# A planner's counts for transfers, instruction fetches and waiting margins are replaced in a hybrid attention layer on one core

## The chip, the cores and the metric

The kernel runs on one core of a Trainium2 chip. The metric is the device time of one execution in microseconds, taken as the median of several runs. The core has a matrix engine (PE in the profile, with PEld for the loading of its stationary operand), a vector engine (DVE), a scalar engine (ACT), a general engine (POOL) and a queue engine (SP) that issues the transfers. Each engine works through its own list of instructions in the order in which the program lists them; between engines they wait on semaphores.

## The reference, cut to what matters

The input x has 512 tokens of 1024 channels. One RMS norm and one wide projection feed two attention mixers and their gates; both mixers are projected, merged with sigmoid gates and projected once more.

```python
h = rms_norm(x, norm_w[l])
proj = h @ w_in[l]
(q_a, k_a, v_a, z_a, q_b, kc, vc, ksl, vsl, kwn, vwn, gate_b, z_b, gate_m) = jnp.split(proj, ...)
o_a = moba_mixer(rms_norm(heads(q_a), ...), rms_norm(heads(k_a), ...), heads(v_a), bias_a)
k_cmp = rms_norm(compress(heads(kc), cmp_pos_k[l], cmp_w1_k[l], cmp_w2_k[l]), k_norm_cmp[l])
v_cmp = compress(heads(vc), cmp_pos_v[l], cmp_w1_v[l], cmp_w2_v[l])
o_b = nsa_mixer(rms_norm(heads(q_b), ...), k_cmp, v_cmp, ksl, vsl, kwn, vwn, gate_b, bias_b)
y_a = o_a * jax.nn.silu(z_a)
y_b = o_b * jax.nn.silu(z_b)
merged = sigmoid(g_m[..., :1024]) * (y_a @ w_branch_a[l]) + sigmoid(g_m[..., 1024:]) * (y_b @ w_branch_b[l])
x = x + merged @ w_out[l]
```

Mixer A (MoBA) has 8 heads of 64 channels; with 512 tokens its two key blocks are both always taken, so that it is causal attention with a bias that depends on the distance. Mixer B (NSA) has 8 heads in 2 groups with three branches: attention to 31 compressed key blocks (`compress` is a two-layer network with 2048 inputs and 256 hidden units), to selected blocks and to a sliding window; here, too, all eight blocks are always selected and the window covers the whole sequence. The three are summed with sigmoid gates.

## The kernel before, in words

**Arithmetic.** Each float32 operand of a large product is split into a high and a low part. A product is three matmul passes: high by high, low by high, high by low. A weight tile of 128x512 comes by a transfer from SP (`dma`, L238) into a raw buffer `wr` (`NRAW` = 6 of them), ACT casts it to the high part `wh` (L402), and DVE subtracts to get the low part `wl` (L412). This is `Stream.split`; the chain of the two steps is listed from the moment at which the planner expects the raw tile to have landed. A second stream of the same class, `W1`, brings the 16 tiles of the compression network (`vh`, `vl`) through two raw buffers.

**Stages.** The projection is worked in pieces: token-major ones with psum tiles `pgt` and channel-major ones with `pgc`, all through `mm3` (matmul at L437). Then come the branch products (`pbr`) and the output products (`po`), through `mm3` as well.

**Attention.** There are 24 units (a pair of heads of one mixer or branch), each with 4 score blocks of up to 512 columns. A score block is two fp16 matmuls into one of two psum buffers `sps` (L1092, L1094). DVE adds the bias and accumulates the maximum (L1114, a custom instruction and a read of the accumulator into `sst`), ACT takes the exponential and the sum (L1125, L1127), DVE takes the reciprocal (L1128), ACT and DVE scale and split into fp16 parts (L1132, L1136), SP sends them through a transposing transfer (`dma_transpose`, L245) into `dst`, and PE multiplies with the values into `O` (24 matmuls, L1168; two more at L1304 add the compressed branch).

**Compressed branch.** The compressed keys and values are gathered from `pgc` (`X`, L912), split into `xs` (L724, L725), and multiplied with the W1 tiles into `hps` (L940). ACT copies the sum to `hs` (L947), PE transposes it into `pu` (L952), and after the second layer the compressed scores `scp` (L1252) follow, with their own softmax `sc` on DVE and ACT (L1257 to L1278, a maximum in `cm` at L1268) and a transpose `pct` (L1291). This happens twice for scores, once for each group of heads.

**The planner.** The order of the instructions on every engine is not written by hand. While the program is built, Python code emulates a clock `now[0]` and times at which each resource is free: `free["A"]`, `free["D"]`, `free["P"]` for the three elementwise engines, `free["S"]` for SP, `free["Q"]` for the transfer engines. Each piece of elementwise work is a `Chain` in a heap, listed when its emulated time comes. PE work comes from ten generators (`Run`): `A` for the score blocks, `O_` and `Y` for the value products and the sides before the output, `F` for the large products, `C` for the compressed branch, `B`, `V`, `Z`, `X`, `U` for preparation. A generator yields either a cost in emulated ns or a readiness; a run may go ahead when its readiness plus its margin (`MARGIN`, or `LATE_A`, `LATE_V`, `LATE_S`, `LATE_C`, `LATE_O`) has passed in the emulated clock, and when none may, the one that has been ready longest goes. Among those eligible, the least served by its share goes. Nothing of this exists on the chip: the chip sees lists of instructions and the semaphores between them. If a wait is real that the planner took to be over, PE stands still, and all that is listed behind stands with it.

The costs that the planner uses for transfers are in `dma` (L236 to L241) and `dma_transpose` (L243 to L247). The matmuls are issued at L437 (`mm3`), L699, L940, L952, L1092, L1094, L1168, L1252, L1304 and a few others, and the planner knows nothing of the fetching of instructions.

Of the kernel before, what the change touches and what calls it, by code (L numbers as in the profile page):

```python
# [108 lines left out]
def hybrid_kernel(ctx: ExitStack, tc: tile.TileContext, x, x0, xT, wtok, wchan, gains, w1,  # L109
# [126 lines left out]
    def dma(dst, src, n, t=None):  # L236

        nc.sync.dma_start(out=dst, in_=src)  # L238
        t = issue(now[0] if t is None else t, 420)
        free["Q"] = max(free["Q"], t + 1000) + max(450, n * P / 360)  # L240
        return free["Q"] + 1700  # L241

    def dma_transpose(dst, src, blocks):  # L243

        nc.sync.dma_start_transpose(out=dst, in_=src)  # L245
        free["Q"] = max(free["Q"], issue(now[0], 1230) + 1500) + blocks * 170
        return free["Q"] + 500  # L247
# [88 lines left out]
    class Stream:  # L336
# [48 lines left out]
        def split(w, upto):  # L385
            for i in range(w.next, min(upto, len(w.tiles))):
                w.next = i + 1
                if isinstance(w.tiles[i], Sum):
                    if i not in w.chain:
                        w.split_sum(i)  # L390
                    continue
                while i not in w.raw:
# [4 lines left out]
                w.out[i] = hi, lo
                c = w.chain[i] = Chain(max(now[0], t))

                def f(e, hi=hi, raw=raw):  # L400
                    if e is nc.scalar:
                        e.copy(hi, raw)  # L402
# [9 lines left out]
                c.do(either(n), lambda e, hi=hi, lo=lo, raw=raw: e.tensor_sub(lo, raw, hi.bitcast(F32))).mark((w, 1, i))  # L412
                c.call(w.load)
# [12 lines left out]
    def mm3(dst, sts, mvs, rows=1, start=True, stop=True, more=False, passes=((0, 0), (1, 0), (0, 1))):  # L426
# [3 lines left out]
        for k in range(0, n, rows):  # L430
# [4 lines left out]
            for a, b in passes:  # L435
                for i in ks:
                    nc.tensor.matmul(dst, sts[i][a], mvs[i][b], start=(start and i == a == b == 0),  # L437
                                     stop=(stop and i == n - 1 and (a, b) == passes[-1]), skip_group_check=more)
# [111 lines left out]
    def x_rms():  # L550
# [5 lines left out]
        for t in range(NT):  # L556
            nc.tensor.matmul(ps[:, t:t + 1], sq_sum[:, t * P:(t + 1) * P], ones, start=True, stop=True)
# [25 lines left out]
    def x_rows():  # L583
# [4 lines left out]
        for i in range(2):  # L588
            nc.tensor.matmul(ps, onesr, dg[i], start=(i == 0), stop=(i == 1))
# [24 lines left out]
    def v_scale(name, tag):  # L614
# [7 lines left out]
        nc.tensor.matmul(ps[:, :1], onesr.bitcast(F32), z[:, KT:KT + 1], start=True, stop=True)  # L622
# [194 lines left out]
    def proj_norm(name, first=False, tags="gggg"):  # L817
        two = []

        def emit(t, ps):  # L820
# [7 lines left out]
            if name == "kb":  # L828
                e_ = sp.tile([P, 24], F32, name=nm("ge"), tag="ge", bufs=3)
# [38 lines left out]
    def bias_rows():  # L868
# [5 lines left out]
        nc.tensor.matmul(ps, *oh, start=True, stop=True)  # L874
# [55 lines left out]
    def compress_h(kv):  # L930
# [4 lines left out]
        for q in range(8):  # L935
            ws = W1.take(1, 256)
            for z in range(2):
                yield ws[0][2].ready
                for i in range(2):
                    nc.tensor.matmul(hps[:, :256], st[2 * q + i], ws[i][z], start=(q == i == z == 0),  # L940
# [10 lines left out]
        for a in range(2):  # L951
            nc.tensor.matmul(ub[:, a * 64:(a + 1) * 64], hs[:, a * P:(a + 1) * P], ii, start=True, stop=True)  # L952
# [51 lines left out]
    def compress_v2(G):  # L1004
        yield room("t")
        ps = psum("t", "pv2")
        for g in range(2):
            for a in range(2):
                nc.tensor.matmul(ps[:, g * 64:(g + 1) * 64], G[:, 2 * a + g].rearrange("p r c -> p (r c)"),
# [31 lines left out]
    class Unit:  # L1041
# [36 lines left out]
        def qk(u, b):  # L1078
# [11 lines left out]
            for x in range(2):  # L1090
                if two:
                    nc.tensor.matmul(sps[:, :n].rearrange("p (h n) -> p h n", h=2), qs, k4[:, x, :, 0], start=not x, stop=bool(x))  # L1092
                else:
                    nc.tensor.matmul(sps[:, :n].rearrange("p (t n) -> p t n", n=P), qs, k4[:, x, j, :b + 1], start=not x, stop=bool(x))  # L1094
# [46 lines left out]
    class Pair:  # L1141
# [15 lines left out]
        def pv(p):  # L1157
# [5 lines left out]
            for kb in (0, 3, 2, 1):  # L1163
                n = S - kb * P
                for vi, pi in ((0, 0), (1, 0), (0, 1)):
                    for r, u in enumerate(p.us):
                        out = o[DH * r:DH * r + DH, S - n:].rearrange("p (b q) -> p b q", q=P)
                        nc.tensor.matmul(out, v[r][kb][:, vi * DH:(vi + 1) * DH], u.moving(kb, pi),  # L1168
# [65 lines left out]
    def nsa_units(g):  # L1234
# [8 lines left out]
        def pre1():  # L1243
# [3 lines left out]
            for i in range(4):  # L1247
# [3 lines left out]
                for b in range(NT):  # L1251
                    nc.tensor.matmul(sps[:, b * DH:(b + 1) * DH], q[:, b * S:b * S + P], kcs[:, g],  # L1252
# [45 lines left out]
        for j in range(2):  # L1298
            def before(o, j=j):
# [3 lines left out]
                for z in range(2):  # L1303
                    nc.tensor.matmul(o, vz[g][:, z].rearrange("p i d -> p (i d)"), ch, start=False, stop=bool(z))  # L1304
# [443 lines left out]
```

## Time and profile before

| | us |
|---|---|
| median of 3 runs | 421.62 |
| the 3 runs | 420.22, 421.62, 422.57 |
| profiled execution | 422.54 |
| its span (first to last instruction) | 420.5 |

| engine | busy us | share of the span |
|---|---|---|
| PE | 411.8 | 98% |
| PEld | 322.0 | 77% |
| DVE | 356.3 | 85% |
| ACT | 297.9 | 71% |
| POOL | 35.1 | 8% |

The engines' busy times overlap, so they do not add up to the span. Matmuls run in a pipeline and their ends are modelled; a short wait between two of them can vanish from the busy time of PE, so the idle times put down to PE and PEld in front of an instruction are read beside the busy share. The granted clock of PE was full in all 40 slices. The 16 transfer engines were busy for 70.5% of the span with the kernel's own transfers.

### The profile page before, as it was taken

The numbers are of one execution on the slowest core, as the hardware profiler recorded it, in microseconds if no ns is written. First come the engines' busy times: TensorE is split into PE (matmuls) and PEld (weight loads), VectorE is DVE, ScalarE is ACT, GpSimd is POOL, SyncE is SP. The second block draws the span as 40 slices with busy tenths as digits, with TensorE's granted clock in tenths as the row PEclk, the third lists the DMA queues.
The fourth block names the chain that finished last, engine by engine and source line by source line (L and its number), as shares of the span: only waits on it lengthen the run. The fifth ranks groups of instructions, "written<-read, shape, count | busy, mean of one in ns | idle before, by whom it ended". The sixth has DMA issues, their size and how long they took to land.

```text
span 420.5 us, 7307 instructions
## 1 busy us (share of the span) xinstructions
PE 411.8 (98%) x2235; PEld 322.0 (77%) x2235; DVE 356.3 (85%) x933; ACT 297.9 (71%) x793; POOL 35.1 (8%) x37
## 2 busy tenths in 40 slices
PE   9999998999998999999999999999999999999996
PEld 7877875778976677897766777666777888888885
DVE  5967969999899987778999997899956967698993
ACT  7996748997797988727988897898943433445620
POOL 0015100123210033200000000000000000000000
PEclk9999999999999999999999999999999999999999
DMA  8951785688969988750878778889799597251232
GB/s 278 311 190 49 129 271 140 137 183 214 264 201 232 195 163 194 218 153 12 147 168 196 150 161 200 167 195 160 145 162 348 175 374 278 79 180 44 56 143 100
DMA packets 116693, 75.30 MB, mean 179 GB/s; under 512 B 89072, under 2 KB 92016, under 8 KB 116656
## 3 DMA queue, kind: packets, MB, share of 16 engines
q1 hardware_dynamic: 116656, 74.86, 70.5%
q8 instruction: 17, 0.28, 0.3%
q14 instruction: 20, 0.16, 0.1%
HBM read 51.11 MB, written 2.75 MB: 128 GB/s over the span
## 4 chain that ended last, share of the span: by engine, by line
PE 54%; DVE 23%; DMA 9%; ACT 5%; issue 5%; SPq 1%; POOL 1%; DVEq 0%; ACTq 0%; POOLq 0%
PE pgc L437 21%; PE pbr L437 9%; PE po L437 9%; PE pgt L437 8%; DMA wr<-in_wtok 5%; DVE sb L1114 4%; DVE wl L412 4%; DVE sb L1136 4%; DMA wr<-in_w 3%; PE O L1168 3%; PE sps L1094 3%; ACT wh L402 2%; DVE vl L412 1%; SPq L238 1%; DMA T<-rtab 1%
## 5 line engine op out<-in xcount | busy, mean ns | idle before, releaser
L437 PE MATMUL pgc<-hh,wh 128*128 128x512 f32 x208 | 87.1, 419 | 0.0
L412 DVE TENSOR_TENSOR wl<-wr,wh 128x512 fp32r<-128x512 f32 (+1 forms) x112 | 73.1, 669 | 11.8 <-ACT wh L402 11.6
L437 PE MATMUL pgc<-hh,wl 128*128 128x512 f32 x208 | 81.5, 392 | 0.0
L437 PE MATMUL pgc<-hl,wh 128*128 128x512 f32 x208 | 81.2, 390 | 0.0
L402 ACT CAST wh<-wr 128x512 fp32r<-128x512 f32 (+1 forms) x111 | 64.0, 599 | 11.2 <-DMA wr<-in_wtok 5.6
L1125 ACT ACTIVATE sb<-sb,sst 128x256 f32<-128x256 f32 (+3 forms) x96 | 53.2, 554 | 10.5 <-DVE sst L1114 10.2
L437 PE MATMUL pgt<-wh,hh 128*128 128x512 f32 (+2 forms) x160 | 58.3, 364 | 0.1
L437 PE MATMUL pgt<-wl,hh 128*128 128x512 f32 (+2 forms) x160 | 56.1, 351 | 0.5 <-DVE wl L412 0.4
L437 PE MATMUL pgt<-wh,hl 128*128 128x512 f32 (+2 forms) x160 | 55.8, 349 | 0.0
L1136 DVE SCALAR_TENSOR_TENSOR sb<-sb,sst 128x256 f16<-128x256 f32 (+3 forms) x96 | 51.1, 542 | 4.2 <-ACT sb L1132 3.9
L1114 DVE CUSTOM_DVE_ANT_0 sb<-sps,T,gst 128x512 f32<-128x512 f32 (+3 forms) x96 | 51.2, 541 | 3.5 <-PE sps L1094 1.6
L1132 ACT ACTIVATE sb<-sb,sst 128x256 f16<-128x256 f32 (+3 forms) x96 | 51.4, 552 | 4.0 <-DVE sst L1128 3.7
L437 PEld LDWEIGHTS pgc<-hh,wh 128*128 128x128 f32 x208 | 39.1, 188 | 8.6 <-issue 0.3
L437 PEld LDWEIGHTS pgc<-hh,wl 128*128 128x128 f32 x208 | 39.0, 188 | 8.6
L437 PEld LDWEIGHTS pgc<-hl,wh 128*128 128x128 f32 x208 | 39.2, 189 | 6.5
L1094 PE MATMUL sps<-qkt,qkt 128*128 128x512 f16 (+3 forms) x176 | 38.2, 310 | 1.6 <-DVE sst L1114 1.4
L489 POOL TENSOR_TENSOR nr<-nss,mhalf 128x8 f32<-128x8 f32 (+1 forms) x16 | 29.0, 1819 | 109.4 <-DVE nss L488 47.9
L437 PEld LDWEIGHTS pgt<-wl,hh 128*128 128x128 f32 x160 | 30.1, 188 | 5.5 <-DVE wl L412 1.6
L437 PEld LDWEIGHTS pgt<-wh,hh 128*128 128x128 f32 x160 | 30.2, 189 | 4.3 <-DVE X L912 0.4
L437 PEld LDWEIGHTS pgt<-wh,hl 128*128 128x128 f32 x160 | 30.2, 189 | 3.4
L1094 PEld LDWEIGHTS <-qkt 128*128 128x128 f16 x176 | 11.5, 98 | 21.4 <-issue 18.5
L437 PE MATMUL pbr<-yh,wh 128*128 128x512 f32 x64 | 26.4, 413 | 0.0
(229 smaller groups left out, 746.3 us busy)
## 6 DMA issues: line engine op xcount, KB each, us to landing
wr<-in_wchan SPq DMA_DIRECT2D x52, 256.0 KB, 3.8
wr<-in_wtok SPq DMA_DIRECT2D x36, 256.0 KB, 4.0
wq<-in_wout SPq DMA_DIRECT2D x36, 256.0 KB, 3.1
T<-rtab SPq DMA_DIRECT2D x16, 256.0 KB, 4.0
wr<-in_w SPq DMA_DIRECT2D x16, 256.0 KB, 3.7
wr<-in_wbr SPq DMA_DIRECT2D x16, 256.0 KB, 3.1
xr<-in_x SPq DMA_DIRECT2D x8, 256.0 KB, 5.3
x<-in_xT SPq DMA_DIRECT2D x7, 256.0 KB, 5.8
```

Of the source, the lines that this page charges most:

```text
L238: nc.sync.dma_start(out=dst, in_=src)
L402: e.copy(hi, raw)
L412: c.do(either(n), lambda e, hi=hi, lo=lo, raw=raw: e.tensor_sub(lo, raw, hi.bitcast(F32))).mark((w, 1, i))
L437: nc.tensor.matmul(dst, sts[i][a], mvs[i][b], start=(start and i == a == b == 0), stop=(stop and i == n - 1 and (a, b) == passes[-1]), ski ...
L489: c.do({"p": 700 + 150 * w}, lambda e: e.tensor_tensor(v(dst), v(ss), mhalf[:parts, :w], op=ALU.pow))
L1094: nc.tensor.matmul(sps[:, :n].rearrange("p (t n) -> p t n", n=P), qs, k4[:, x, j, :b + 1], start=not x, stop=bool(x))
L1114: e.tensor_tensor_reduce(z["sb"], sps[:, :L], T[:, S - L:], scale=nrunscale, scalar=3e38, op0=ALU.add, op1=ALU.min, accum_out=st[:, 0, b:b ...
L1125: c.do({"A": 279 + 0.834 * L}, lambda e: e.activation(z["sb"], z["sb"], AF.Exp, bias=st[:, 0, b:b + 1], scale=-1.0, accum_out=st[:, 1, b:b ...
L1132: e.activation(z["pp"][:, :L], z["sb"], AF.Copy, scale=s_)
L1136: c.do({"d": 59 + cd(L)}, lambda e: e.scalar_tensor_tensor(z["pp"][:, L:], z["sb"], s_, z["pp"][:, :L], op0=ALU.mult, op1=ALU.subtract))
L1168: nc.tensor.matmul(out, v[r][kb][:, vi * DH:(vi + 1) * DH], u.moving(kb, pi), start=p.first and kb == vi == pi == 0, stop=p.last and kb == ...
```

## The change

The change alters numbers of the planner, one helper around the matmul, and the shape and count of one small tile. No instruction is added or removed: each engine issues as many of each kind as before, in another order. All matmuls go through the new helper `mm`, so that they share one line (L261), and lines behind it move down by 17 (L412 becomes L429, L1114 becomes L1131, L1136 becomes L1153, L912 becomes L929).

```diff
-MARGIN = 300
-LATE_A = 1000
+MARGIN = 450
+LATE_A = 750
 LATE_V = 2000
 LATE_S = 1000
-LATE_C = 300
+LATE_C = 1000
 LATE_O = 1000
-LATE_Y = 1000
+LATE_Y = 2000
...
+SQ_L = 560
+SQ_T = 1330
+DQ_L = 1540
+DE_L = 800
+DQ_T = 1370
+DE_T = 1200
+FETCH = 1200
+LAND = 500
+LAND1 = 1500
...
     def dma(dst, src, n, t=None):
 
         nc.sync.dma_start(out=dst, in_=src)
-        t = issue(now[0] if t is None else t, 420)
-        free["Q"] = max(free["Q"], t + 1000) + max(450, n * P / 360)
-        return free["Q"] + 1700
+        t = issue(now[0] if t is None else t, SQ_L)
+        free["Q"] = max(free["Q"], t + DQ_L) + max(300, n * P / 314)
+        return free["Q"] + DE_L
 
     def dma_transpose(dst, src, blocks):
 
         nc.sync.dma_start_transpose(out=dst, in_=src)
-        free["Q"] = max(free["Q"], issue(now[0], 1230) + 1500) + blocks * 170
-        return free["Q"] + 500
+        free["Q"] = max(free["Q"], issue(now[0], SQ_T) + DQ_T) + blocks * 145
+        return free["Q"] + DE_T
+
+    fetched = [0]
+
+    def mm(*a, **k):
+        nc.tensor.matmul(*a, **k)
+        fetched[0] += 2
+        if (fetched[0] + 90) % 256 < 2:
+            free["Q"] = max(free["Q"], now[0]) + FETCH
...
-                c = w.chain[i] = Chain(max(now[0], t))
+                c = w.chain[i] = Chain(max(now[0], t + (LAND1 if w is W1 else LAND)))
...
-                    nc.tensor.matmul(dst, sts[i][a], mvs[i][b], start=(start and i == a == b == 0),
+                    mm(dst, sts[i][a], mvs[i][b], start=(start and i == a == b == 0),
...
-                e_ = sp.tile([P, 24], F32, name=nm("ge"), tag="ge", bufs=3)
+                e_ = sp.tile([P, 34], F32, name=nm("ge"), tag="ge", bufs=4)[:, :24]
```

The replacement of `nc.tensor.matmul` by `mm` stands at all the other matmuls, too. In words: SP's time for one issue is counted as 560 instead of 420 ns (1330 instead of 1230 for a transposing one); the transfer engines are counted as 300 ns at least for one transfer and as 314 instead of 360 bytes per ns; the landing comes 800 instead of 1700 ns behind them (1200 instead of 500 for a transposing one); with each 128 matmuls the transfer engines are counted as taken for 1200 ns; a weight tile's cast is listed 500 ns behind its counted landing, 1500 ns for W1; and four margins change.

From about 300 us of matrix work on, PE's list is the same in both. What moves lies ahead of it. Three places are shown; the numbers behind a name tell one buffer from the next, and the names of the two programs do not share their numbers.

The first place is DVE's list where the score blocks of the second unit start, while token-major products run. Before:

```order
L912 TENSOR_TENSOR X_873<-pgc_766,R 64x256
L1136 SCALAR_TENSOR_TENSOR sb_804<-sb_804,sst_729 128x256
L1136 SCALAR_TENSOR_TENSOR sb_809<-sb_809,sst_729 128x128
L412 TENSOR_TENSOR wl_858<-wr_736,wh_857 128x512
L412 TENSOR_TENSOR wl_860<-wr_751,wh_859 128x512
L912 TENSOR_TENSOR X_873<-pgc_766,R 64x256
L412 TENSOR_TENSOR wl_862<-wr_758,wh_861 128x512
L1114 ISA sb_901,sst_833<-sps_889,T_723,gst 128x256
L1114 ISA sst_833 128x1
L1114 ISA sb_903,sst_833<-sps_894,T_723,gst 128x128
L1114 ISA sst_833 128x1
L412 TENSOR_TENSOR wl_864<-wr_772,wh_863 128x512
```

With the change, at the same place (from the same `X` on):

```order
L929 TENSOR_TENSOR X_870<-pgc_763,R 64x256
L429 TENSOR_TENSOR wl_854<-wr_739,wh_853 128x512
L429 TENSOR_TENSOR wl_856<-wr_750,wh_855 128x512
L429 TENSOR_TENSOR wl_858<-wr_767,wh_857 128x512
L929 TENSOR_TENSOR X_870<-pgc_763,R 64x256
L429 TENSOR_TENSOR wl_860<-wr_779,wh_859 128x512
L1131 ISA sb_898,sst_830<-sps_887,T_726,gst 128x256
L1131 ISA sst_830 128x1
L1131 ISA sb_900,sst_830<-sps_892,T_726,gst 128x128
L1131 ISA sst_830 128x1
L1153 SCALAR_TENSOR_TENSOR sb_798<-sb_798,sst_732 128x256
L1153 SCALAR_TENSOR_TENSOR sb_811<-sb_811,sst_732 128x128
```

Before, two scalings into fp16 (L1136) came first, then three low parts `wl`, the bias of two score blocks and the fourth `wl`; now the four `wl` come first, then the bias, and the scalings (L1153) last.

The second place is PE's list between the last product of the first hidden sum `hps` and the transpose `pu` that reads its copy `hs`. Before:

```order
L940 MATMUL hps_1130<-vl_1704,xs_765 128x256 x2
L1094 LDWEIGHTS qkt_959
L1094 MATMUL sps_1854<-qkt_961,qkt_959 128x384
L1094 LDWEIGHTS qkt_959
L1094 MATMUL sps_1854<-qkt_961,qkt_959 128x384
L437 MATMUL pgc_1776<-hh,wh_1616 128x512
L437 MATMUL pgc_1776<-hl,wh_1616 128x512
L437 MATMUL pgc_1776<-hh,wl_1617 128x512
L437 MATMUL pgt_1878<-wh_1625,hh 128x512
L437 MATMUL pgt_1878<-wh_1625,hl 128x512
L437 MATMUL pgt_1878<-wl_1626,hh 128x512
L952 MATMUL pu_1893<-cst,hs_1853 128x64 x2
```

With the change, the rows just ahead of `pu` are these; ahead of them stand the last `hps` products, one more score block (512 columns) and the first half of the one whose second half is shown:

```order
L261 LDWEIGHTS qkt_938
L261 MATMUL sps_2012<-qkt_940,qkt_938 128x384
L261 MATMUL pgt_1928<-wh_1825,hh 128x512
L261 MATMUL pgt_1928<-wh_1825,hl 128x512
L261 MATMUL pgt_1928<-wl_1826,hh 128x512
L261 MATMUL pgt_2030<-wh_1583,hh 128x512
L261 MATMUL pgt_2030<-wh_1583,hl 128x512
L261 MATMUL pgt_2030<-wl_1584,hh 128x512
L261 MATMUL pgt_2030<-wh_1593,hh 128x512
L261 MATMUL pgt_2030<-wh_1593,hl 128x512
L261 MATMUL pgt_2030<-wl_1594,hh 128x512
L261 MATMUL pu_2049<-cst,hs_2005 128x64 x2
```

One score block and six matmuls of 512 columns stood between the last `hps` and `pu` before; two score blocks and nine such matmuls stand there now.

The third place is DVE's list around the compressed softmax of the second group of heads, at its maximum `cm`. Before it stands beside the score blocks number 43 and 44 of the 96:

```order
L1114 ISA sb_2931,sst_2926<-sps_2921,T_2610,gst 128x512
L1114 ISA sst_2926 128x1
L1136 SCALAR_TENSOR_TENSOR sb_2775<-sb_2775,sst_2720 128x128
L1128 RECIPROCAL sst_2771<-sst_2771 128x1
L1268 TENSOR_REDUCE cm_2888<-sc_2798 128x16
L412 TENSOR_TENSOR wl_2940<-wr_2751,wh_2939 128x512
L1128 RECIPROCAL sst_2771<-sst_2771 128x1
L1114 ISA sb_2957,sst_2926<-sps_2949,T_2610,gst 128x384
L1114 ISA sst_2926 128x1
L1366 TENSOR_TENSOR zs_2868<-pgc_2869,R 128x512
L1269 TENSOR_TENSOR sc_2798<-sc_2798,cm_2888 128x512
```

With the change the same reduction stands beside score block number 60, 91 rows of DVE's list further on:

```order
L1275 TENSOR_TENSOR sc_3231<-sc_3231,scp_3316 128x128
L1153 SCALAR_TENSOR_TENSOR sb_3244<-sb_3244,sst_3130 128x128
L1153 SCALAR_TENSOR_TENSOR sb_3134<-sb_3134,sst_3067 128x128
L1131 ISA sb_3369,sst_3302<-sps_3360,T_2854,gst 128x256
L1131 ISA sst_3302 128x1
L1153 SCALAR_TENSOR_TENSOR sb_3247<-sb_3247,sst_3130 128x384
L1145 RECIPROCAL sst_3302<-sst_3302 128x1
L1285 TENSOR_REDUCE cm_3323<-sc_3231 128x16
L1153 SCALAR_TENSOR_TENSOR sb_3280<-sb_3280,sst_3130 128x256
L1396 TENSOR_TENSOR gm_3263<-pgc_3264,R 128x512
L1145 RECIPROCAL sst_3302<-sst_3302 128x1
L1286 TENSOR_TENSOR sc_3231<-sc_3231,cm_3323 128x512
```

The four compressed score tiles of that group and their softmax have moved from the stretch of score blocks 32 to 52 into the stretch of 52 to 70; none of DVE's rows is gone or new.

More of the change, by code (lines that the diff above doesn't have):

```diff
@@ L507, in hybrid_kernel @@
     for _ in range(NWARM):
-        nc.tensor.matmul(pw[:, :P], warm[:, :1].to_broadcast([P, P]), warm[:, :1].to_broadcast([P, P]), start=True,
+        mm(pw[:, :P], warm[:, :1].to_broadcast([P, P]), warm[:, :1].to_broadcast([P, P]), start=True,
                          stop=True)
@@ L556, in x_rms @@
         for t in range(NT):
-            nc.tensor.matmul(ps[:, t:t + 1], sq_sum[:, t * P:(t + 1) * P], ones, start=True, stop=True)
+            mm(ps[:, t:t + 1], sq_sum[:, t * P:(t + 1) * P], ones, start=True, stop=True)
             yield 214
@@ L588, in x_rows @@
         for i in range(2):
-            nc.tensor.matmul(ps, onesr, dg[i], start=(i == 0), stop=(i == 1))
+            mm(ps, onesr, dg[i], start=(i == 0), stop=(i == 1))
         yield cm(S) * 2
@@ L621, in v_scale @@
         ps = psum(tag, "psv")
-        nc.tensor.matmul(ps[:, :1], onesr.bitcast(F32), z[:, KT:KT + 1], start=True, stop=True)
+        mm(ps[:, :1], onesr.bitcast(F32), z[:, KT:KT + 1], start=True, stop=True)
         yield 214
@@ L873, in bias_rows @@
         ps = psum("t", "pR")
-        nc.tensor.matmul(ps, *oh, start=True, stop=True)
+        mm(ps, *oh, start=True, stop=True)
         yield cm(S)
@@ L939, in compress_h @@
                 for i in range(2):
-                    nc.tensor.matmul(hps[:, :256], st[2 * q + i], ws[i][z], start=(q == i == z == 0),
+                    mm(hps[:, :256], st[2 * q + i], ws[i][z], start=(q == i == z == 0),
                                      stop=(q == 7 and i == z == 1))
@@ L951, in compress_h @@
         for a in range(2):
-            nc.tensor.matmul(ub[:, a * 64:(a + 1) * 64], hs[:, a * P:(a + 1) * P], ii, start=True, stop=True)
+            mm(ub[:, a * 64:(a + 1) * 64], hs[:, a * P:(a + 1) * P], ii, start=True, stop=True)
         yield 300
@@ L976, in compress_k2 @@
         for a in range(2):
-            nc.tensor.matmul(ps[:64, :64], G[:, a * 64:(a + 1) * 64], w2t[:, 0, a, :], start=(a == 0), stop=(a == 1))
+            mm(ps[:64, :64], G[:, a * 64:(a + 1) * 64], w2t[:, 0, a, :], start=(a == 0), stop=(a == 1))
         yield 300
@@ L1008, in compress_v2 @@
             for a in range(2):
[L1009 removed]
+                mm(ps[:, g * 64:(g + 1) * 64], G[:, 2 * a + g].rearrange("p r c -> p (r c)"),
                                  w2t[:, 1, a, :], start=(a == 0), stop=(a == 1))
@@ L1091, in qk @@
                 if two:
-                    nc.tensor.matmul(sps[:, :n].rearrange("p (h n) -> p h n", h=2), qs, k4[:, x, :, 0], start=not x, stop=bool(x))
+                    mm(sps[:, :n].rearrange("p (h n) -> p h n", h=2), qs, k4[:, x, :, 0], start=not x, stop=bool(x))
                 else:
-                    nc.tensor.matmul(sps[:, :n].rearrange("p (t n) -> p t n", n=P), qs, k4[:, x, j, :b + 1], start=not x, stop=bool(x))
+                    mm(sps[:, :n].rearrange("p (t n) -> p t n", n=P), qs, k4[:, x, j, :b + 1], start=not x, stop=bool(x))
             yield 2 * max(3 + 0.417 * n, 60)
@@ L1251, in pre1 @@
                 for b in range(NT):
-                    nc.tensor.matmul(sps[:, b * DH:(b + 1) * DH], q[:, b * S:b * S + P], kcs[:, g],
+                    mm(sps[:, b * DH:(b + 1) * DH], q[:, b * S:b * S + P], kcs[:, g],
                                      start=True, stop=True)
@@ L1303, in before @@
                 for z in range(2):
-                    nc.tensor.matmul(o, vz[g][:, z].rearrange("p i d -> p (i d)"), ch, start=False, stop=bool(z))
+                    mm(o, vz[g][:, z].rearrange("p i d -> p (i d)"), ch, start=False, stop=bool(z))
                 yield 2 * cm(S)
```

4 lines of the change are left out of this document (2 added, 2 removed).

## The prediction

> **What bounds the kernel now.** First the page's busy times and the windows (20 us each: busy time and count of PE, PEld, DVE, ACT, POOL, then the granted clock, the transfers' share, GB/s).
>
> ```profile
> PE 411.8 (98%) x2235; PEld 322.0 (77%) x2235; DVE 356.3 (85%) x933; ACT 297.9 (71%) x793; POOL 35.1 (8%) x37
> 60.00:80.00 20.00, 18.28 (x84) 12.38 (x83) 19.61 (x62) 16.65 (x54) 0.00 (x0) 1.00 0.62 158
> 120.00:140.00 20.00, 18.53 (x94) 13.86 (x93) 19.63 (x60) 17.44 (x53) 1.01 (x1) 1.00 1.04 233
> 200.00:220.00 20.00, 20.00 (x113) 14.26 (x111) 20.00 (x65) 18.05 (x53) 0.00 (x0) 1.00 0.84 161
> 220.00:240.00 20.00, 19.94 (x131) 13.89 (x130) 19.73 (x60) 17.34 (x54) 0.00 (x0) 1.00 0.84 177
> 240.00:260.00 20.00, 19.77 (x108) 14.35 (x108) 17.33 (x57) 17.31 (x52) 0.00 (x0) 1.00 0.76 166
> 260.00:280.00 20.00, 20.00 (x127) 13.71 (x126) 18.48 (x58) 18.67 (x55) 0.00 (x0) 1.00 0.84 167
> 340.00:360.00 20.00, 20.00 (x90) 16.57 (x89) 12.34 (x22) 6.16 (x13) 0.00 (x0) 1.00 0.78 273
> ```
>
> PE is the bound: 98% busy at full clock. Its list has the same matmuls after the change, so time can come only from the places where PE stands. In 340:360 there is none. The two windows with most idle are 60:80 (20 − 18.28 = 1.72 us) and 120:140 (1.47 us); both have DVE above 98%. So DVE's order matters there, since a value that DVE delivers late has no idle DVE time to be caught up in.
>
> How much one matmul costs PE is read from the chain of waits (start, time, what): 24 passes of 512 columns follow each other in 5.44 us, 0.227 us each; a set of 24 value products takes 1.75 us and two compressed ones 0.66.
>
> ```profile
> 311.06 5.44 PE pgc L437 x24
> 316.50 1.75 PE O L1168 x24
> 318.25 0.66 PE O L1304 x2
> ```
>
> Then the waits of PE and its weight loader over the whole span (line, releaser, us in total, times, longest).
>
> ```profile
> PEld pu L952 <- ACT hs L947: 1.8, 1, 1.8
> PEld pgt L437 <- DVE wl L412: 1.6, 3, 0.8
> PEld L1168 <- DMA dst<-sb: 1.4, 2, 1.1
> PEld hps L940 <- DVE vl L412: 0.4, 1, 0.4
> PEld pgt L437 <- DVE X L912: 0.4, 1, 0.4
> PE sps L1094 <- DVE sst L1114: 1.4, 2, 1.1
> PE pu L952 <- ACT hs L947: 1.3, 1, 1.3
> PE O L1168 <- DMA dst<-sb: 0.8, 1, 0.8
> PEld L1094 <- issue: 18.5, 65, 1.2
> ```
>
> PEld's named waits are 1.8 + 1.6 + 1.4 + 0.4 + 0.4 = 5.6 us, and the score blocks' 1.4 on PE makes 7.0. That is all that a better order can win by name. (The 18.5 us on "issue" ahead of 65 score-block loads name no producer, and the change removes no such load.)
>
> **The stretch from 60 to 80 us.** Two of the three waits for a low part fall into 55 to 80 us (first row, the waits of that window); DVE's timeline shows two scalings ahead of these low parts.
>
> ```profile
> PEld pgt L437 <- DVE wl L412: 1.4, 2, 0.8
> 67.36 0.73 DVE L1136 SCALAR_TENSOR_TENSOR sb<-sb,sst 128x256 f16<-128x256 f32 x2
> 68.02 1.28 DVE L412 TENSOR_TENSOR wl<-wr,wh 128x512 fp32r<-128x512 f32 x2
> 72.84 0.75 DVE L1114 CUSTOM_DVE_ANT_0 sb<-sps,T,gst 128x512 f32<-128x512 f32 x1
> ```
>
> The scalings take 0.73 us, and their reader is a transposing transfer whose products come much later. PE waits for the two low parts behind them, then for an X, and then at 73 us a score block waits for a free psum buffer, which the bias at 72.84 had not yet read. The changed list puts four low parts first, the bias behind them, and the scalings last. I count PE's whole idle time of that window as gone: **−1.7 us**. The ends are 0 (the low parts come earlier but the bias is still late, since DVE is full) and −2.9 (low parts 1.4 of the 1.6, X 0.4, score block 1.1).
>
> **pu.** PE reached pu while ACT was late with the copy hs.
>
> ```profile
> 130.22 0.62 ACT L402 CAST vh<-wr 128x512 fp32r<-128x512 f32 x1 [2.34 <-DMA wr<-in_w]
> 130.49 0.40 PE L940 MATMUL hps<-vl,xs 128*128 128x256 f32 x2
> 130.73 0.50 PE L1094 MATMUL sps<-qkt,qkt 128*128 128x384 f16 x2
> 133.53 0.35 ACT L947 COPY hs<-hps 128x256 f32<-128x256 f32 x1
> 133.94 0.66 PE L952 MATMUL pu<-cst,hs 128*128 128x64 f32 x4 [1.32 <-ACT hs L947]
> ```
>
> The copy is late because ACT, which works in order, stood 2.34 us for a W1 tile that had not landed, and 11 other operations then stood ahead of the copy. Two edits bear on it. LAND1 lists that cast 1.5 us later, and LATE_C (1000 for 300) makes the planner wait longer before pu. By the order, one more score block and three more matmuls stand between the last hps and pu: 3 × 0.227 = 0.7, and 0.4 to 0.5 for the block (0.50 for the two passes of 384 columns above, 512 in the new one): about 1.1 of cover. **−1.1 us**; the ends are 0 and −1.8.
>
> **The value products.** At 146.67 us a set of value products starts, and after one of them the rest has not arrived.
>
> ```profile
> 143.81 2.49 SPq L245 DMA_TRANSPOSE dst<-sb  x2
> 147.86 1.44 PE L1168 MATMUL O<-dst,v 128*64 128x512 f16 x19 [0.79 <-DMA dst<-sb]
> ```
>
> The transpose lands some 1.5 us after SP's queue has done issuing it (143.81 + 2.49 to 147.86). The planner counted 500 ns from the transfer's end to its landing and now counts 1200, and it counts 1330 instead of 1230 for the issue. The matmuls between this unit's last score block and its first value product come to 18.3 us at the rates above before, and to 23.4 us after: 5 us more against a wait of 0.8 to 1.1. **−0.8 us**; ends 0 and −1.1.
>
> **The small waits.** hps for vl 0.4, the third low part 0.2, the other score block 0.3 and the rest of O's 0.3: 1.2 us, of which I take less than half, since each is found at another place once the order has moved: **−0.5 us**, ends 0 and −1.2.
>
> **What the transfer counts themselves do.** A weight tile was counted as landing 1000 + 728 + 1700 = 3.43 us after its issue; now 1540 + 835 + 800 = 3.18, plus 0.5 before its cast is listed, 3.68.
>
> ```profile
> wr<-in_wchan SPq DMA_DIRECT2D x52, 256.0 KB, 3.8
> wr<-in_wtok SPq DMA_DIRECT2D x36, 256.0 KB, 4.0
> wr<-in_w SPq DMA_DIRECT2D x16, 256.0 KB, 3.7
> q8 instruction: 17, 0.28, 0.3%
> ```
>
> The measured medians are 3.7 to 4.0 us, so the new count is nearer. This matters only where ACT stands with something urgent behind it; elsewhere ACT (71%) has room. Nothing is charged beyond the waits above. The fetches of instructions (q8) are 17 packets that took 0.3% of 16 engines over 420.5 us: 0.003 × 16 × 420.5 / 17 = 1.19 us each, on one engine of 16. FETCH counts the same 1.2 us for all 16 together, so it errs towards later conversions. [...] The tile ge is a few bytes and is charged nothing; its cover is ACT's room, and without that one 24-column exponential would wait.
>
> **The cost that the change adds.** The second group's compressed scores and softmax now stand between score blocks 52 and 70. Between DVE's reads of these two stand 103 rows before and 126 after (accumulator reads included). In 200:240 a full DVE does 65 + 60 rows in 39.73 us, 0.318 each: 32.8 us before, 40.1 after. PE has 117 passes × 0.227 = 26.6, value products 1.75 + 1.75 + 0.66 = 4.2, 18 score blocks at about 0.33 (estimated from the 0.50 for 384 columns) = 6, and about 1 of small ones: 37.8. So DVE has 2.3 us more work than PE there. Behind block 70 stand some 5 us of products without a new block, in which DVE catches up. The bounds are 0 (200:240, DVE full, PE loses 0.06 of 40 us) and +3 (the 2.3, and a late softmax of 0.7 behind it). By the nearest row, 200:240, I take **+0.5 us**.
>
> **The sum.** −1.7 − 1.1 − 0.8 − 0.5 + 0.5 = −3.6 us. The profiled execution took 422.54 us (span 420.5 and 2.04 around it), 0.9 above the median of 421.62; 3.6 less is 418.9 for it and **418.0** for the median.
>
> **The rivals.** A measurement of this kernel tells 0.5%, 2.1 us, from no change.
>
> Refilled: DVE is the true bound where PE stood, so its own idle time is all that the first two terms can win: 0.39 in 60:80 and 0.37 in 120:140 instead of 2.8. Then −0.76 − 0.8 − 0.5 + 0.5 = −1.6, 420.0. For it speaks DVE's 98% in both windows; against it, that most rows moved ahead there are only swapped with rows that nobody waits for. This is also what happens if the new counts do not hit the waits. Chance 0.22.
>
> Slower: the stretch of blocks 52 to 70 becomes DVE's, and DVE is not even full in it, because it waits for ACT and PE in the chain of bias, exponential, reciprocal and scaling. In 240:280 DVE stood 2.67 + 1.52 = 4.2 of 40 us. With that, the stretch lasts 40.1 + 4.2 = 44.3 instead of 37.8, +6.5, and with −4.1 of gains the median comes to 424.0. It decides from about 3.9 us of DVE idle time in that stretch (2.3 + 3.9 − 4.1 = 2.1). For it, 240:280; against it, 200:240, where DVE stood 0.3 of 40. Chance 0.12.
>
> More: all 7.0 us of named waits go and nothing is added: 414.6. Chance 0.04. [...]
>
> **How the numbers follow.** The forecast has 0.62, with a range of its own from 415.1 (the far ends of the gains, −2.9 − 1.8 − 1.1 − 1.2 = −7.0, and +0.5) to 419.5. The range asked for takes in the refilled case too, up to 422.6 (the gains of that case gone and 1 us of the added cost): 415.1 to 422.6. Outside are the slower case, the largest gain, and a tail of the refilled one. Faster 0.66, same 0.22, slower 0.12.
>
> **What would show it.** In the changed profile the waits of pu for hs, O for dst, and pgt for wl between 60 and 80 us should be gone, and PE's idle time in 60:80 and 120:140 below 0.5. DVE should be near 20 of 20 from about 215 to 255 us, with PE's waits on sst there below 1 us. The forecast is wrong if PE's idle time comes back as waits for other producers in the same windows (refilled), or if sps waits for sst by several us around the second group (slower).

## The result

The changed kernel took 417.25 us (median of four executions; 416.93 without the longest of them) against 421.52 for the one before, a ratio of 0.9889 with a 95% interval of 0.9859 to 0.9918. Measured again in run e1, it took 417.88 against 421.68: 0.9911 (0.9890 to 0.9931). The forecast was 418.0. One of the first four executions, the profiled one, took 826 us, with PE busy for 820.1 us on the same 2235 matmuls, so the profile after is that of e1: 417.20 us, span 415.0.

### The profile page after: what moved, and what is told of

Read it like the earlier page. It is cut to its first block, busy times and chain, and to the rows that moved or that the text cites. A ratio compares the mean times of both kernels' runs of the same rounds, so it can differ in the third digit from the quotient of the medians.

```text
span 824.2 us, 7296 instructions
## 1 busy us (share of the span) xinstructions
PE 820.1 (99%) x2235; PEld 524.6 (64%) x2235; DVE 362.8 (44%) x932; ACT 305.1 (37%) x794; POOL 32.7 (4%) x37
## 4 chain that ended last, share of the span: by engine, by line
PE 99%; DVE 0%; issue 0%; POOL 0%; POOLq 0%
PE pgc L261 35%; PE pgt L261 22%; PE pbr L261 11%; PE po L261 10%; PE sps L261 7%; PE O L261 6%; PE pgf L261 5%; PE hps L261 2%; PE pw L261 1%; PE pct L1308 0%; PE scp L261 0%; PE pv L261 0%; PE pu L261 0%; PE pss L261 0%; PE prx L261 0%; PE psv L261 0%
## 5 line engine op out<-in xcount | busy, mean ns | idle before, releaser
L261 PE MATMUL pgc<-hh,wh 128*128 128x512 f32 x208 | 149.6, 719 | 0.0
L261 PE MATMUL pgc<-hh,wl 128*128 128x512 f32 x208 | 140.7, 676 | 0.0
L261 PE MATMUL pgc<-hl,wh 128*128 128x512 f32 x208 | 140.5, 676 | 0.0
L1131 DVE CUSTOM_DVE_ANT_0 sb<-sps,T,gst 128x512 f32<-128x512 f32 (+3 forms) x96 | 51.8, 548 | 129.5 <-PE sps L261 128.9
L261 PE MATMUL pgt<-wh,hh 128*128 128x512 f32 (+2 forms) x160 | 95.7, 598 | 0.0
L261 PE MATMUL pgt<-wl,hh 128*128 128x512 f32 (+2 forms) x160 | 93.8, 586 | 0.0
L261 PE MATMUL pgt<-wh,hl 128*128 128x512 f32 (+2 forms) x160 | 93.5, 584 | 0.0
L429 DVE TENSOR_TENSOR wl<-wr,wh 128x512 fp32r<-128x512 f32 (+1 forms) x112 | 73.2, 667 | 31.5 <-ACT wh L419 14.2
L261 PEld LDWEIGHTS pgc<-hh,wl 128*128 128x128 f32 x208 | 62.7, 302 | 33.2 <-issue 30.3
L261 PEld LDWEIGHTS pgc<-hh,wh 128*128 128x128 f32 x208 | 64.1, 308 | 30.0 <-issue 25.6
L261 PEld LDWEIGHTS pgc<-hl,wh 128*128 128x128 f32 x208 | 63.0, 303 | 27.2 <-issue 25.1
L261 PE MATMUL sps<-qkt,qkt 128*128 128x256 f16 (+3 forms) x184 | 71.4, 510 | 0.0
L261 PEld LDWEIGHTS pgt<-wh,hh 128*128 128x128 f32 x160 | 51.6, 322 | 15.9 <-issue 13.0
L261 PEld LDWEIGHTS pgt<-wl,hh 128*128 128x128 f32 x160 | 49.8, 311 | 16.0 <-issue 13.8
L261 PEld LDWEIGHTS pgt<-wh,hl 128*128 128x128 f32 x160 | 49.8, 311 | 13.8 <-issue 12.8
L261 PEld LDWEIGHTS <-qkt 128*128 128x128 f16 x216 | 21.2, 152 | 53.1 <-issue 50.1
L1153 DVE SCALAR_TENSOR_TENSOR sb<-sb,sst 128x256 f16<-128x256 f32 (+3 forms) x96 | 50.6, 539 | 1.3 <-ACT sb L1149 1.0
L261 PE MATMUL pbr<-yh,wh 128*128 128x512 f32 x64 | 46.2, 722 | 0.0
L261 PE MATMUL pbr<-yl,wh 128*128 128x512 f32 x64 | 43.3, 676 | 0.0
```

The source lines that it names most:

```text
L261: nc.tensor.matmul(*a, **k)
L1131: e.tensor_tensor_reduce(z["sb"], sps[:, :L], T[:, S - L:], scale=nrunscale, scalar=3e38, op0=ALU.add, op1=ALU.min, accum_out=st[:, 0, b:b ...
L1153: c.do({"d": 59 + cd(L)}, lambda e: e.scalar_tensor_tensor(z["pp"][:, L:], z["sb"], s_, z["pp"][:, :L], op0=ALU.mult, op1=ALU.subtract))
```

## The profile after

First the page's busy times and the head of the chain of work that ended last, of the kernel before and then of the changed one.

```profile
PE 54%; DVE 23%; DMA 9%; ACT 5%; issue 5%; SPq 1%; POOL 1%; DVEq 0%; ACTq 0%; POOLq 0%
```

```profile
PE 409.7 (99%) x2235; PEld 321.4 (77%) x2235; DVE 353.0 (85%) x932; ACT 298.4 (72%) x794; POOL 36.4 (9%) x37
...
PE 88%; DVE 6%; DMA 2%; issue 2%; ACT 1%; SPq 0%; POOL 0%; DVEq 0%; POOLq 0%
```

The chain ran through other engines for almost half of its length before, and through PE for 88% now. (One operation that DVE had before is with ACT now: 932 for 933, and 794 for 793. So the lists differ by a little more than their order.) Then the windows of 20 us (columns as in the prediction), first one row and the sum over 0 to 320 us of the kernel before, then those of the changed one.

```profile
140.00:160.00 20.00, 19.21 (x109) 14.92 (x108) 18.43 (x62) 18.25 (x55) 4.44 (x4) 1.00 0.87 171
...
sum 320.00, PE 314.55 PEld 241.49 DVE 275.61 ACT 256.43 POOL 35.08; mean PE 19.66 PEld 15.09 DVE 17.23 ACT 16.03 POOL 2.19
```

```profile
60.00:80.00 20.00, 19.21 (x90) 13.28 (x90) 19.59 (x62) 16.82 (x54) 0.70 (x1) 1.00 0.64 152
...
120.00:140.00 20.00, 20.00 (x99) 15.79 (x98) 19.93 (x62) 19.34 (x62) 1.01 (x1) 1.00 1.03 224
140.00:160.00 20.00, 20.00 (x115) 15.79 (x113) 18.43 (x58) 18.97 (x57) 8.77 (x4) 1.00 0.91 182
...
200.00:220.00 20.00, 20.00 (x125) 14.06 (x124) 20.00 (x66) 17.64 (x52) 0.00 (x0) 1.00 0.86 190
220.00:240.00 20.00, 20.00 (x129) 14.62 (x127) 19.21 (x63) 17.61 (x53) 0.00 (x0) 1.00 0.77 171
240.00:260.00 20.00, 19.76 (x123) 13.52 (x123) 19.31 (x61) 17.63 (x51) 0.00 (x0) 1.00 0.74 145
...
sum 320.00, PE 318.05 PEld 245.15 DVE 277.96 ACT 260.63 POOL 36.40; mean PE 19.88 PEld 15.32 DVE 17.37 ACT 16.29 POOL 2.27
```

Over these 320 us PE stood 5.45 us before and 1.95 after: 3.50 less, beside the 3.6 of the forecast and the 3.8 to 4.6 between the medians. (The two profiled executions lie 5.3 apart, 422.54 and 417.20; each is towards the outer end of its kernel's scatter, so their difference says too much. What the idle time leaves of it, some 2 us, is in PE's busy time, 411.8 and 409.7 us for the same matmuls. Short waits can vanish in that (in `before`, at 340 us, matmuls recorded as 0.39 us long start 0.23 us apart), and which they were stays open.) Where it went: 0.93 in 60:80, 1.47 in 120:140, 0.79 in 140:160, and 0.3 in the rest. The waits of PE between 20 and 320 us, the span's start left out, are two:

```profile
PE pgt L261 <- ACT nraw L789: 0.8, 1, 0.8
PE sps L261 <- DVE sst L1131: 0.2, 1, 0.2
```

The waits of pu for hs and of O for dst are gone. The first row is new, and it stands in 60:80. The weight loader still waits there for low parts, 0.7 us where it was 1.4:

```profile
PEld pgt L261 <- DVE wl L429: 0.7, 2, 0.5
```

The timeline of the new wait:

```profile
69.20 0.69 DVE L429 TENSOR_TENSOR wl<-wr,wh 128x512 fp32r<-128x512 f32 x1
69.81 0.48 DVE L1131 CUSTOM_DVE_ANT_0 sb<-sps,T,gst 128x256 f32<-128x256 f32 x1
...
70.33 0.51 ACT L1142 ACTIVATE sb<-sb,sst 128x256 f32<-128x256 f32 x1 [0.83 <-DVE sst L1131]
...
71.32 0.67 ACT L789 ACTIVATE nraw<-pgt,rx 128x512 f32<-128x512 f32 x1
...
72.04 0.50 PE L261 MATMUL pgt<-wh,hh 128*128 128x512 f32 x1 [0.78 <-ACT nraw L789]
```

The low parts come first now, as the order showed. But the bias of the score blocks comes no earlier for that: it starts 0.54 us ahead of PE's next score block in both kernels (70.39 and 70.93 before, 69.81 and 70.35 now). ACT's exponential waits 0.83 us for it, and the reading of a finished projection (nraw) stands behind that exponential in ACT's list. PE needs its psum buffer and waits 0.78. On PE this one wait stands where 0.4 us for a low part and 1.1 us for the bias stood before.

## The experiments

All times are medians beside executions of the kernel before on the same chip (421.4 to 421.7 us).

### The parts of the change (e1 to e4)

Theory N says that the gain is the sum of the named waits, so that each part is worth the waits that its order covers. Theory D says that DVE's load sets PE's pace wherever PE stood. e1 is the changed kernel unaltered. The edits of the other three, on the kernel before (e2) and on the changed one (e3, e4):

```diff
 e2
-MARGIN = 300
+MARGIN = 450
-LATE_A = 1000
+LATE_A = 750
-LATE_C = 300
+LATE_C = 1000
-LATE_Y = 1000
+LATE_Y = 2000
 e3
-MARGIN = 450
+MARGIN = 300
-LATE_A = 750
+LATE_A = 1000
-LATE_C = 1000
+LATE_C = 300
-LATE_Y = 2000
+LATE_Y = 1000
 e4
-LAND = 500
-LAND1 = 1500
+LAND = 0
+LAND1 = 0
```

> The changed kernel once more, unaltered, for a profile at PE's usual pace and a tighter interval. Theory N (named waits; the sum of the prediction): 417 to 418.5 us; PE stands under 0.5 us in 60:80 and in 120:140, the waits of pu for hs and of O for dst are gone, and at most 0.5 us of waits on sst is new between 200 and 270 us. Theory D (DVE's load sets PE's pace wherever PE stood): about the same time, but PE stands for some 1.7 us in all between 205 and 250 us, because DVE's list there is 2.3 us longer than PE's.

> The kernel before with the four new margins alone (MARGIN 450, LATE_A 750, LATE_C 1000, LATE_Y 2000). By the order, the cover of pu rises from 1.7 to 6.5 us of matmuls and that of the third set of value products from 18.3 to 21.3, while DVE's list around 60 to 75 us stays as before. Theory N: pu's 1.3 and the value products' 0.8 go, the 1.7 of 60:80 stay: 419.4 us (420.0 at most). Theory D: DVE's work up to 150 us is no shorter against PE's (it comes out 3.3 us behind, 2.6 before), so the waits only move: 421 to 422.5.

> The changed kernel with the four margins of before (so the counts of transfers, fetches and landings, and the tile ge). By the order, pu's cover is 2.1 us (1.7 before), the third value products' 21.7 (18.3). Theory N: 60:80 loses 1.0 less, pu 0.4, value products 0.8, small ones 0.4: 2.6 less, 418.9 us. Theory D: a new pile of DVE work around 105 us puts DVE 3.1 us behind PE, as far as before in all: 421 to 422.

> The changed kernel with LAND and LAND1 at 0. By the order, pu's cover is 3.1 us, the third value products' 19.4, DVE's list at 60 to 75 us is as tight as before. Theory N: 1.3 and 0.5 and 0.2 gone, 60:80 as before: 419.5 us. Theory D: DVE is 3.1 us behind PE by 150 us: 421 to 422. Apart from both, if casts that stand waiting for a tile hold up ACT, waits of ACT for wr or of vh for wr are longer than in the changed kernel by 2 us or more in all.

Measured: e1 417.88 (0.9911), e2 428.70 (1.0168, 1.0141 to 1.0196), e3 420.25 (0.9964, 0.9945 to 0.9983), e4 424.76 (1.0073, 1.0048 to 1.0098). So the margins alone cost 7.0 us, the counts alone win 1.4, together they win 3.8. On e1 N is right in the time and in pu and O, though PE stood 0.79 us in 60:80 where N had under 0.5; the 1.7 us that D expected between 205 and 250 us did not come. e3 lies between the two (418.9 for N, 421 to 422 for D): the waits for hs and dst are gone from PE's list there, and 2.3 us for sst (1.4 before) and 0.8 for vl (0.2 before) stand in it, at other places. Both theories fail on e2 and e4: N had both faster than before, and D had at most 422.5 us. N's bookkeeping forgets that a list in which some waits are covered has others. In e2, the largest of these:

```profile
132.87 0.62 DVE L1131 CUSTOM_DVE_ANT_0 sb<-sps,T,gst 128x384 f32<-128x384 f32 x1 [3.57 <-DMA dst<-sb]
...
133.54 0.27 PE L261 MATMUL sps<-qkt,qkt 128*128 128x128 f16 x2 [2.69 <-DVE sst L1131]
```

DVE is not full here. It stands 3.57 us, because the bias writes into a buffer `sb` that a transposing transfer has not finished reading; PE then waits 2.69 us for a psum buffer that this bias was to free. In e4 the same 2.69 us stand ahead of a score block at 138.77, with another cause: DVE has no idle time from 130.66 to 138.63, and the bias that is to free the buffer comes late in its full list, at 138.10. The casts that were listed too early do not show as the expectation had it: ACT's waits for the tiles of wr are 4.5 us in all, against 5.2 in the changed kernel.

```profile
138.10 0.60 DVE L1131 CUSTOM_DVE_ANT_0 sb<-sps,T,gst 128x384 f32<-128x384 f32 x1
...
138.77 0.27 PE L261 MATMUL sps<-qkt,qkt 128*128 128x128 f16 x2 [2.69 <-DVE sst L1131]
```

### A margin that stands for a count (e5, e6)

The wait in e2 suggests theory C: LATE_A had hidden that the planner takes the buffers of bias results to be free too early. Theory M blames the other margins. e5 is the kernel before with one number changed, e6 the changed kernel with the two landing margins and FETCH at 0.

```diff
 e5
-LATE_A = 1000
+LATE_A = 750
 e6
-FETCH = 1200
-LAND = 500
-LAND1 = 1500
+FETCH = 0
+LAND = 0
+LAND1 = 0
```

> The kernel before with one number changed, LATE_A 750 for 1000 (how long the planner lets a score block's free buffers age before it lists the block). Theory C (a margin stands for what the counts leave out; with the old counts of transposing transfers the planner believes the buffers of bias results free about 0.6 us too early, and 1000 hid that): nearly the whole loss of the four margins alone, 427 to 429.5 us, with DVE waiting 5 us or more in all for dst<-sb. Theory M (the other margins, LATE_C above all, moved the compressed branch into a bad place, and LATE_A does no harm): 421 to 423 us, DVE's waits for dst near the 1.4 us of before.

> The changed kernel without FETCH, LAND and LAND1 (all 0): the four margins and the counts of issue, queue and landing. Theory C: the counts take the harm out of the margins; DVE waits under 2 us for dst, 421 to 423.5 us, no better than before, since the casts are listed too early still. Theory M: 426 us or more, as with the margins alone.

Measured: e5 428.30 (1.0167, 1.0130 to 1.0204), e6 423.35 (1.0051, 1.0031 to 1.0071). DVE's waits for transposes, in the lists of waits of the kernel before, e2, e5 and e6:

```profile
DVE sb L1114 <- DMA dst<-sb: 1.4, 3, 0.7
```

```profile
DVE sb L1131 <- DMA dst<-sb: 7.9, 7, 3.6
```

```profile
DVE sb L1131 <- DMA dst<-sb: 7.6, 7, 2.1
```

```profile
DVE sb L1131 <- DMA dst<-sb: 2.5, 2, 1.6
```

The one number brings the whole loss of e2 and as much waiting; with the new transfer counts most of it is gone, though 2.5 us is more than the 2 that C allowed. M falls. C holds in the main: LATE_A 750 costs some 7 us with the old counts and does not with the new ones. That it is the transposes' landing alone which does it is argued and not shown, since e6 has the new counts of direct transfers, too; and e6 is still 1.9 us slower than before.

### Is it the fetches? (e7)

The records of single transfers in the first nine traces let the count of 1200 ns be measured. For each transfer from issue to landing, those in flight during an instruction fetch (q8), and as a control those in flight 8 us ahead of or behind one:

```
                 at a fetch: n, median us    8 us from one: n, median us
dst<-sb                138, 4.13                  347, 3.17
wr<-in_wchan            87, 4.65                  222, 3.77
wr<-in_wtok            121, 5.00                   75, 3.85
wr<-in_w                27, 4.26                   61, 3.43
T<-rtab                 34, 4.64                   61, 3.88
wr<-in_wbr              21, 4.71                   63, 4.45
wq<-in_wout             37, 4.91                  147, 4.83
```

Transposes and the projections' weight tiles land 0.9 to 1.15 us later when they are in flight at a fetch, other kinds 0.1 to 0.8. The control has other transfers at other places of the program. Set against the same transfer (same kind, same number within its kind) in those of the thirteen traces of `before` and e1 to e12 in which no fetch met it, the ones at a fetch land 1.2 us later (dst, 197 of them), 1.0 (in_wtok, 86), 0.9 (in_wchan, 99) and 0.5 (wq, 19), in the median. Whether counting that is what wins, is asked by e7.

```diff
-FETCH = 1200
+FETCH = 100
```

> The changed kernel with FETCH 100 for 1200 (the planner no longer holds transfers up at an instruction fetch). Theory P (FETCH is spare time that happens to move the lists well; walking the changed lists with the durations of the traces, without any fetch, gives 4 us more for this one): 420.5 to 423 us, and PE's new waits are for DVE and ACT with no transfer behind them that landed late. Theory F (real fetches hold transfers up by 1.2 us): also slower, 419 to 421, but with new waits of ACT for wr or of DVE for dst of 2 us or more against the changed kernel. If FETCH does nothing: 417.9.

The walk named there, and below, is a reckoning of mine that no profile shows: each engine's list is gone through in order, each instruction starts when the one ahead and the semaphores allow it, with the median durations of the first five traces and the transfer times of the changed planner. No fetch is in it.

Measured: 421.54 (1.0003, 0.9987 to 1.0020), 3.7 us more than e1, inside the range of P and outside that of F. PE's waits in e7:

```profile
PE sps L261 <- DVE sst L1131: 1.8, 4, 0.9
PE pgt L261 <- DVE wl L429: 1.3, 1, 1.3
```

The second is at 136.75 us. In 120 to 160 us ACT waits for no tile in e7, and the nearest fetches are at 114.2 and 140.2; DVE has had no gap since 130.86, and four low parts in a row come too late. So the largest wait has no fetch in it. One of F's signs is there: ACT waits 2.62 us for a tile at 164.75, behind the fetch at 161.2. DVE waits 2.79 and 1.96 us for ACT behind it, and PE 0.58 us for DVE at 170.92. So up to some 0.6 of the 3.7 us can be a fetch's. The fetches are real, but most of what FETCH is worth here comes from the order that it happens to give.

### Has DVE room where the softmax went? (e8, e12)

The same edit in the changed kernel (e8) and in the one before (e12): four more maxima for the second group, with the same result.

```diff
-            cc.do({"D": 600}, lambda e: e.reduce_max(m, s3, axis=AX.X))
+            cc.do({"D": 600}, lambda e: [e.reduce_max(m, s3, axis=AX.X) for _ in range(5 if g else 1)][-1])
```

> The changed kernel in which the maximum of the second group's compressed scores is taken five times in a row on DVE (four more of about 0.6 us, the same result; the planner doesn't know of them). They stand in the stretch of score blocks 52 to 70. Theory D (DVE is at its limit there, as the prediction's added cost of 0.5 us supposes, and has nothing left): +2 to +3 us, 420 to 421, with PE standing for sst between 215 and 260 us. If DVE had room there: within 0.7 us of 417.9.

> The kernel before with the same four further maxima in the second group's compressed softmax, which stands beside score blocks 43 and 44 there. Theory D (DVE has no room at that place either): 2 to 3 us more, 423.5 to 424.7, so the move of the softmax put the same burden at another place. If only the changed kernel's stretch is at DVE's limit, as the added cost of the prediction had it: within 0.7 us of 421.6.

Measured: e8 420.31 (0.9971, 0.9955 to 0.9987), 2.4 more than e1 (2.7 when each is taken against the kernel before on its own chip); e12 424.04 (1.0059, 1.0037 to 1.0081), 2.4 more than the kernel before. The rows of e8, then those of e12:

```profile
241.90 3.55 DVE L1285 TENSOR_REDUCE cm<-sc 128x16 f32<-128x512 f32 x5
...
246.58 0.47 PE L261 MATMUL pgc<-hh,wh 128*128 128x512 f32 x1 [2.42 <-DVE sst L1145]
```

```profile
213.12 3.55 DVE L1268 TENSOR_REDUCE cm<-sc 128x16 f32<-128x512 f32 x5
...
217.92 0.27 PE L1094 MATMUL sps<-qkt,qkt 128*128 128x128 f16 x2 [1.68 <-DVE sst L1114]
```

Five maxima take 3.55 us, so four add about 2.9, and 2.4 to 2.7 of these come out at the end. Theory D holds at this place: DVE has next to no room in either stretch. The change carried the softmax from one full stretch into another. The trace of e1 shows how near the limit that is. These are the first and the last score block of the stretch from 52 to 70, on PE and then, at its bias, on DVE:

```profile
219.89 0.50 PE L261 MATMUL sps<-qkt,qkt 128*128 128x384 f16 x2
258.18 0.61 PE L261 MATMUL sps<-qkt,qkt 128*128 128x512 f16 x2
221.02 0.62 DVE L1131 CUSTOM_DVE_ANT_0 sb<-sps,T,gst 128x384 f32<-128x384 f32 x1
263.29 0.75 DVE L1131 CUSTOM_DVE_ANT_0 sb<-sps,T,gst 128x512 f32<-128x512 f32 x1
```

PE needs 38.3 us from the one to the other and DVE 42.3, so DVE falls back from 1.1 to 5.1 us behind PE. In the kernel before it needs 37.1 us for the stretch.

### How much hangs on the one list? (e9 to e11)

Theory T: the gain comes from counts that are near the truth, so a count moved a little further or nearer does nothing. Theory S: it belongs to one list that came out well. Edits on the changed kernel:

```diff
 e9
-DE_L = 800
+DE_L = 700
 e10
-FETCH = 1200
+FETCH = 1000
 e11
-DE_T = 1200
+DE_T = 1400
-LATE_Y = 2000
+LATE_Y = 1500
```

> The changed kernel with DE_L 700 for 800: direct transfers are counted as landing 0.1 us earlier, a fortieth of what they take. Theory T (the gain comes from counts that are near the truth): nothing to tell, 417.2 to 418.6 us. Theory S (the gain belongs to one list that came out well; any number that reorders it costs some of it): 420 to 423 us (walking this list with the durations of the traces gives 4 us more than the changed one), with new waits of PE for DVE around 100, 170 and 215 us.

> The changed kernel with FETCH 1000 for 1200, which is nearer to the 1.0 us by which transfers in flight at a fetch landed later in the traces. Theory T: as the changed kernel or better, 417 to 418.2 us. Theory S: another list, so worse: 418.5 to 420.5 (the walk gives 1.2 more).

> The changed kernel with DE_T 1400 for 1200 and LATE_Y 1500 for 2000, the best of some sixty single and double neighbours by the walk (1.1 us less than the changed list). If the walk tells such lists apart: 416 to 417.3 us, all of it after 200 us and in the stretch from 120 to 160. If it can't at this size: 417 to 419.

Measured: e9 419.99 (0.9956, 0.9934 to 0.9979), e10 418.77 (0.9936, 0.9910 to 0.9962), e11 416.74 (0.9871, 0.9845 to 0.9896). e9 is 2.1 us above e1 for 0.1 us in one count: outside what T allowed and just below the 420 to 423 of S. Its new waits:

```profile
PE pgt L261 <- DVE vb L873: 1.0, 1, 1.0
...
PE O L261 <- DMA dst<-sb: 0.7, 1, 0.7
PE pgt L261 <- DVE wl L429: 0.5, 2, 0.3
```

Those for wl are near 100 us and that for vb is at 174, as the walk had them; the one of O at 313 it had not, and what it had at 215 did not come. e10 lies with S, but its interval and e1's overlap. Yet T is not all wrong: e9 and e10 are still faster than before. e11 is the fastest kernel here. Its six executions (416.03 to 416.93) lie below the six of e1 (417.20 to 418.48), but three executions of the changed kernel in the first measurement (416.37 to 417.56) reach among them, so a gain of e11 over the change is a hint and not shown. Nor does it show as idle time where the walk had it: PE stands for nothing in 120:160 in e1 already, and from 200 to 320 us it stands for 0.08 us in e11 and 0.26 in e1.

Differences from the kernel before, in us, of the walk and as measured:

```
            e1    e2    e3    e4    e5    e6    e7    e8    e9    e10   e11   e12
walk       -4.8  +6.6  -2.9  +2.6  +7.1  +0.5  -0.5  -1.8  -0.6  -3.6  -5.9  +2.9
measured   -3.8  +7.0  -1.4  +3.1  +6.9  +1.9  +0.1  -1.1  -1.7  -2.9  -4.9  +2.4
```

Durations and waits alone thus come within 1.5 us of each, and give the sign of each but e7, which measures no difference. Of these values those for e7, e9, e10 and e11 were put down, rounded, ahead of their runs; for the others that is not on record.

## Why the prediction was right, point by point

**60:80, −1.7 forecast.** Measured −0.93. Of the named waits the score block's 1.1 us went, and the weight loader's 1.4 for low parts fell to 0.7 where all of it was to go. The term's own near end (the low parts come earlier but the bias is late) came half true: the bias was as late as before, and showed up as a wait for ACT's nraw. This is the refilled rival, in one window. PE's idle time of 0.79 there missed the sign that it would be below 0.5.

**pu, −1.1.** Measured −1.47 in 120:140, all that PE stood there. The wait went as a whole; DVE rose from 19.63 to 19.93 of 20 us meanwhile, so DVE's own idle time did not cap the gain, as the refilled rival had it.

**Value products, −0.8.** Measured −0.79 in 140:160.

**Small waits, −0.5.** Measured about −0.3.

**Added cost, +0.5.** Measured 0: in 200:280 PE stood 0.29 us before and 0.26 after. DVE was as full as forecast in the first 20 us of the stretch (20.00) and less so behind it (19.21 and 19.31 where near 20 was forecast). The sum of this term had PE at 37.8 us and DVE at 40.1; they took 38.3 and 42.3. So DVE did fall behind, by 4.0 us where 2.3 were reckoned, and the fault of the term is the step from there to a loss: PE's list had enough other products in between, and none came out. There was no room to spare, as e8 shows, nor was there before, as e12 shows. The slower rival was near to being right: 2.9 us of further DVE work called up 2.4 to 2.7 of it.

**FETCH.** The step "on one engine of 16 … so it errs towards later conversions" failed. Set against the same transfer without a fetch, those in flight at one land 1.2, 1.0 and 0.9 us later in three of the four kinds compared (0.5 in the fourth), and 1200 is close to that. On PE no wait is put down to a fetch. That nothing was charged for FETCH was wrong, too: without it the gain was gone (e7, 421.54 us), though mostly by the order and not by the fetches.

**What was luck.** The waits named were the right ones, but no term but the value products came out within 0.1 us: 60:80 gave 0.8 us less than forecast and the small waits 0.2 less, pu gave 0.4 more and the added cost 0.5 less. These errors cancel to 0.1, which nothing in the working promised.

**What the prediction did not say.** It took the change for a sum of parts. The sum of the waits was right only since it was read from the one finished list; the same reckoning applied to parts of the change (theory N in e2 and e4) was wrong by 9 and 5 us. The chance of 0.12 for slower was about that one list's stretch of DVE work, and nothing in it priced that a single margin of this change costs 7 us by itself.

## What to carry to other kernels

Where a planner orders the work, a margin may stand for something that its counts leave out: correct the count before the margin is cut, and look for the cut one's damage in buffers that a transfer still reads. Predict such a change from the finished lists, place by place, with durations from a trace; in these runs the changed numbers themselves did not tell even the sign. When a wait is removed, follow the next link on the engines that were full, since there a part of it may come back under another name (0.78 of 1.72 us here).

## What the runs showed of the hardware

A gap of PE can cost more than itself. Behind the 2.69 us gap of e2 the granted clock fell; the windows of 2 us (PE busy, granted clock, transfers) of e2, then of e4 behind its gap of the same length:

```profile
134.00:136.00 2.00, 2.00 (x7) 0.61 0.87 161
136.00:138.00 2.00, 2.00 (x6) 0.54 1.01 310
138.00:140.00 2.00, 2.00 (x12) 1.00 1.07 279
```

```profile
138.00:140.00 2.00, 1.23 (x7) 1.00 0.78 165
140.00:142.00 2.00, 2.00 (x11) 1.00 0.98 202
```

In e2 that is 0.39 × 2 + 0.46 × 2 = 1.7 us lost, as of 3.4 us at half the clock. e5 shows the same behind a gap of 2.54 us: the granted clock is 0.50 in 142:144 and 0.65 in 144:146, again 1.7 us lost. Behind the gaps of e4 (2.69 us) and e8 (2.42) it stays at 1.00. So 1.7 us of what e2 loses is the clock's, as an estimate from these rows. The length of the gap does not tell the cases apart, and what does is not shown. Where a gap falls may decide. In the records of the granted clock, 129.71, 3.41 and 290.13 us lie between the changes in e2, 136.53, 3.41 and 283.31 in e5, and 416.43 in `before`, which are 38, 1, 85, 40, 1, 83 and 122 times 3.413 us. If such steps are counted from the first rise of the clock in the other traces, too, which is an estimate of mine from these three, then 2.5 us of e2's gap and all 2.54 of e5's lie within one step, while the end of a step cuts e4's gap into 1.9 and 0.8 us and e8's into 1.5 and 0.9. These are four cases, and no run was made to test it. It fits that the same kernel can do either: four of e4's six executions and four of e8's ten have a mean granted clock of 0.995 or 0.996, as all six of e2's have, though where their gaps fell is not on record.

The other thing not expected is the effect of an instruction fetch on transfers in flight, 1.2, 1.0, 0.9 and 0.5 us in the four kinds compared, shown ahead of the measured time of e7.
